# A third raw weight buffer, and g_final loaded into the output ring, in a one-layer hybrid encoder kernel

## The chip, the cores and the metric

The kernel runs on one core of one Trainium2 chip. A core has a matrix engine (TensorE, in the profile PE, with its weight loads as PEld), a vector engine (VectorE, DVE), a scalar engine (ScalarE, ACT), a general engine (GpSimd, POOL), and a queue engine (SyncE, SP) that in this kernel issues all transfers. Each engine carries out its own list of instructions in order and waits on semaphores for the others. The metric is the time of one execution on the device in microseconds, given as the median of several runs.

## What is computed

One inference step of a one-layer encoder over 2048 prompt tokens and 32 sample tokens that have 128 cached tokens before them. The model width is 1024, all numbers are fp32:

```python
a = rmsnorm(x, g_attn)
qa, ka, va, qb, kb, vb = split(a @ w_in)              # six parts of 512 columns
oa = softmax(q1 k1) v - lam * softmax(q2 k2) v        # group A: 4 heads, two maps, T5 bias, 64-chunk causal
ob = softmax(q k + clip bias) v                       # group B: 8 heads, own chunk and 8 chunks before
h = x + concat(rmsnorm(oa, subln_g) * c, rmsnorm(ob, out_norm_b)) @ w_out
h = h + square(relu(rmsnorm(h, g_mlp) @ w_up)) @ w_down          # 4096 wide
h = h + sigmoid(h @ w_ple_gate) * (p @ w_ple_proj)
y = rmsnorm(h, g_final)                               # outputs: y, and the new keys and values
```

The last line is the one that uses `g_final`: a vector of 1024 numbers, multiplied onto every token's row.

## The kernel before

**Tokens and precision.** The 2080 tokens are worked on in four blocks: 0, 1 and 2 of 512 tokens and 3 of 544 (its last 32 are the sample). To reach fp32 accuracy on TensorE, every operand is split into a high and a low part, and a product is three matmuls (`mm3`, L164 to L170): high weight by high activation (L168), high weight by low activation (L169), low weight by high activation (L170).

**Weights.** All weights are streamed in slices of 128 x 1024 numbers (512 KB, or 4 KB in each of the 128 partitions). `wunit` (L155) fetches one slice: a raw tile `wr` is loaded by SyncE, ScalarE copies it to the high part `wh` (L149), and GpSimd subtracts to get the low part `wl` (L153). There are 338 such slices in the run. The tiles come from rings: `wr` has two buffers, `wh` and `wl` three each. A raw buffer is free for the next load when both the copy and the subtraction of its slice are done; a `wh` or `wl` buffer is free when TensorE has finished the last matmul with it.

**Stages.** In order: normalisation and projection of blocks 0 and 1 (`prep`, `proj`, w_in); first half of attention A (`attn_a`, L516); projection and band attention (`attn_b`, L650) side by side; second half of attention A, into whose gaps the output projection (`outproj`, L818, w_out) and the MLP (`mlp`, L899 to L960, w_up and w_down) of blocks 0 and 1 are woven; then gate (`gate`, L966) and final norm (`final`, L1017) of block 1; output projection of blocks 2 and 3; gate and final norm of block 0; the MLP of blocks 2 and 3, which is nearly pure matrix work; and gate and final norm of blocks 2 and 3 at the end. In the profile, matmuls carry the names of their outputs: `qps` for w_in, `ops` for w_out, `ups` and `dps` for w_up and w_down, `gps` and `pps` for the gate, `s` for the scores of attention A (L545).

In attention A, keys (`ka`), queries (`q`) and values (`v`) are loaded from scratch memory in HBM for each head and group of queries. Its normed outputs `os` (L645) are stored back to HBM as `oT`.

**What sets the order.** All engines' instruction lists are written by a scheduler: the program is given to a tile framework (L1269) that places every instruction by priorities, buffers and a model of the times. A change of one buffer count can therefore move instructions on every engine. On the chip each list is then carried out in order, whatever the true times are. All transfers are issued by one line (`dma`, L139 to L144) on SyncE, so they stand in one queue: a transfer that has to wait for its buffer or its data holds back all transfers behind it.

**The final norm.** `final` is called four times, for the blocks 1, 0, 2 and 3 in this order. For each 128 tokens it transposes the block's hidden state on TensorE, copies it to a tile `yn` of 128 x 512 for each half of the columns (the last call uses the PSUM tile and an output tile `yo` for the second half), sums the squares into a throw-away tile `junk`, and multiplies by the row's scale and by `g_final` (L1054); then `yn` is stored. The tiles `yn`, `yo` and `junk` come from a ring of activation tiles with the tag "u": for block 1 the ring `uq` with 8 slots of 2 KB per partition, afterwards the ring `uh` with 16 slots. `g_final` lies in a tile `gf` of 128 x 1024 (4 KB per partition), the same row in each partition. `gfin` (L962) loads it, once into the pool `fk` before the second half's output projection (L1164), and once more into a new pool after block 1 is done (L1206).

Of the kernel before, what the change touches and what calls it, by code (L numbers as in the profile page):

```python
# [12 lines left out]
F32 = mybir.dt.float32  # L13
# [6 lines left out]
P = 128  # L20
D = 1024
# [12 lines left out]
BLK = 544  # L34
# [10 lines left out]
def toks(b):  # L45
    out = []
    for i in range(4):
        out.append((i * P, P))
    if b == 3:
        out.append((512, SS))  # L50
    return out
# [81 lines left out]
class Kern:  # L133
# [20 lines left out]

    def wunit(self, src, shape, hi_eng="act", lo_eng="pool"):  # L155
        nc = self.nc
        raw = self.wp.tile([P] + shape, F32, tag="wr", bufs=2, name="wr")
        self.dma(raw, src)
        hi = self.wp.tile([P] + shape, F32R, tag="wh", bufs=3, name="wh")
        lo = self.wp.tile([P] + shape, F32R, tag="wl", bufs=3, name="wl")  # L160
        self.split(hi, lo, raw, hi_eng, lo_eng)
        return hi, lo
# [796 lines left out]
            prev = us  # L959
        self.mlp_down(ch, nf, blocks, prev, st, wk, md)  # L960

    def gfin(self, pool):  # L962
        self.gf = pool.tile([P, D], F32, name="gf")
        self.dma(self.gf, self.a["g_final"].unsqueeze(0).broadcast_to([P, D]))

    def gate(self, b, h, up, act, md):  # L966
        nc, a = self.nc, self.a
        n, t0 = BN[b], 512 * b
# [48 lines left out]
    def final(self, b, h, up, fk, mm, md=None):  # L1017
        nc, a = self.nc, self.a
        t0 = 512 * b
        sts, yns = {}, {}  # L1020
        phased = md is not None

        def side(c0, tn, q):
            if phased:
                sts[c0] = st_all[:, c0 // P]
            elif q == 0:
                sts[c0] = fk.tile([P, 2], F32, tag="fst", bufs=6, name="fst")
            st = sts[c0]
            yp = (md if phased and q == 1 else mm).tile([P, 512], F32, tag="mm", name="yp")
            for k in range(4):  # L1030
                nc.tensor.transpose(yp[:tn, P * k : P * k + P], h[:, 4 * q + k, c0 : c0 + tn], self.ident)
            if phased and q == 1:
                yns[c0, q] = yp
            else:
                yns[c0, q] = up.tile([P, BLK], F32, tag="u", name="yn")[:, :512]
                nc.vector.tensor_copy(yns[c0, q][:tn], yp[:tn])
            junk = up.tile([P, BLK], F32, tag="u", name="junk")[:tn, :512]
            nc.scalar.activation(junk, yp[:tn], AF.Square, accum_out=st[:tn, q : q + 1])

        if phased:  # L1040
            st_all = fk.tile([P, 5, 2], F32, tag="fsa", name="fsa")
            nc.gpsimd.memset(st_all, 1.0)
            for c0, tn in toks(b):
                side(c0, tn, 0)
                yield
        def emit(c0, tn, r):
            tt = t0 + c0
            dst = a["y_prompt"][0, tt : tt + tn] if tt < SP else a["y_sample"][0, tt - SP : tt - SP + tn]
            for q in range(2):
                src = yn = yns[c0, q]  # L1050
                if phased and q == 1:
                    yn = up.tile([P, BLK], F32, tag="u", name="yo")[:, :512]
                g = self.gf[:tn, 512 * q : 512 * q + 512]
                nc.vector.scalar_tensor_tensor(yn[:tn], src[:tn], r, g, op0=ALU.mult, op1=ALU.mult)  # L1054
                self.dma(dst[:, 512 * q : 512 * q + 512], yn[:tn])

        if phased:
            for c0, tn in toks(b):
                side(c0, tn, 1)
            ss = fk.tile([P, 5], F32, tag="fss", name="fss")  # L1060
            nc.vector.tensor_tensor(ss, st_all[:, :, 0], st_all[:, :, 1], op=ALU.add)
            r = self.rsqrt(fk, ss, 5, 1.0 / D, EPS, nc.vector, "rfa")
            for i, (c0, tn) in enumerate(toks(b)):
                emit(c0, tn, r[:tn, i : i + 1])
            return
        for c0, tn in toks(b):
            side(c0, tn, 0)
            side(c0, tn, 1)
            st = sts[c0]
            nc.vector.tensor_tensor(st[:tn, 0:1], st[:tn, 0:1], st[:tn, 1:2], op=ALU.add)  # L1070
            emit(c0, tn, self.rsqrt(fk, st[:tn, 0:1], 1, 1.0 / D, EPS, nc.vector, "rf", tn, 5))
            yield

    def run(self):
        tc, nc, a = self.tc, self.nc, self.a
        with ExitStack() as top:

            def opened(stack, name, bufs, space=None, side="left"):
                kw = {} if space is None else {"space": space}
                return stack.enter_context(  # L1080
                    tc.tile_pool(name=name, bufs=bufs, side=side, reuse_waits="tile", **kw)
                )
# [31 lines left out]
            with ExitStack() as x:  # L1114
                pool = opened(x, "a0", 1, side="right")
# [42 lines left out]
            with ExitStack() as x:  # L1158
                pool = opened(x, "a1", 1, side="right")
# [1 line left out]
                    self.attn_a(js, pool, ps_s, ps_t, ps_o)  # L1161
            wk = opened(sq_, "wk", 1)
            fk = opened(sq_, "fk", 1)
            self.gfin(fk)  # L1164
            acc, cn, st = {}, {}, {}
            def norms(b, act, ps):
                self.colnorm(acc[b][0], b, 1.0 / D, wk, ps, "mm", self.rS)
# [10 lines left out]
            up = Sized(opened(top, "uh", 16, side="right"), BLK)  # L1178
# [24 lines left out]
            psx.close()  # L1203
            wk = opened(top, "wk4", 1)
            fk = opened(top, "fk4", 1)
            self.gfin(fk)  # L1206
            md = opened(top, "md", 8 - MM, PSUM, "right")
            act = Sized(opened(top, "acth", 4), BLK, True)
            hh = opened(top, "hh", 2, side="right")
# [1 line left out]
            g = self.outproj(3, wk, oa[3], md, acc[3])  # L1211
# [4 lines left out]
            g = self.gate(0, h, up, act, md)  # L1216
# [12 lines left out]
            g = self.gate(3, st[3][0], up, act, md)  # L1229
# [54 lines left out]
```

## Time and profile before

| | us |
|---|---|
| median of 3 runs | 3329.38 |
| lowest and highest run | 3328.49, 3332.86 |
| the profiled execution | 3334.02 |
| its span on the core | 3332.1 |

The mean granted clock of TensorE in the profiled execution was 0.969 of full speed. The profiled execution took 1.9 us beyond its span.

How the page is read: the busy table gives each engine's busy time, its share of the span and the number of its instructions. A group line names the source line, the engine, the operation and output<-input tiles, then the count, the busy total in us, the mean ns of one, and the idle time of the engine before these instructions with what ended most of it. A line of waits names who waited for whom, with the total in us, the number of times, and the longest. A line of the timeline begins with the start and the duration in us, and x2 means that two like instructions are merged into it; on SyncE a duration is that of issuing, together with waits between merged issues.

### The profile page before, as it was taken

The numbers are of one execution on the slowest core, as the hardware profiler recorded it, in microseconds if no ns is written. First come the engines' busy times: TensorE is split into PE (matmuls) and PEld (weight loads), VectorE is DVE, ScalarE is ACT, GpSimd is POOL, SyncE is SP. The second block draws the span as 40 slices with busy tenths as digits, with TensorE's granted clock in tenths as the row PEclk, the third lists the DMA queues.
The fourth block names the chain that finished last, engine by engine and source line by source line (L and its number), as shares of the span: only waits on it lengthen the run. The fifth ranks groups of instructions, "written<-read, shape, count | busy, mean of one in ns | idle before, by whom it ended". The sixth has DMA issues, their size and how long they took to land.

```text
span 3332.1 us, 50114 instructions
## 1 busy us (share of the span) xinstructions
PE 3111.6 (93%) x17881; PEld 2723.4 (82%) x17881; DVE 1674.4 (50%) x3952; ACT 1705.5 (51%) x3717; POOL 1467.9 (44%) x1083
## 2 busy tenths in 40 slices
PE   6988989999999999989899999988989999999998
PEld 6877778889877888778787878877779999999987
DVE  5117777454555544566656665746542322223235
ACT  4226666566665666666666665654443223222245
POOL 4335654432324433534544443555753333333365
PEclk9998899999999999999999999999999999999999
DMA  7488777786788554544644454346631111111133
GB/s 227 160 253 235 214 212 202 213 241 205 209 238 234 159 139 126 143 137 133 197 134 123 129 136 130 121 135 222 181 114 51 45 45 45 45 47 49 45 91 102
DMA packets 519074, 488.93 MB, mean 147 GB/s; under 512 B 37885, under 2 KB 414017, under 8 KB 518825
## 3 DMA queue, kind: packets, MB, share of 16 engines
q1 hardware_dynamic: 518824, 485.73, 50.2%
q8 instruction: 142, 2.33, 0.3%
q14 instruction: 108, 0.88, 0.1%
HBM read 379.06 MB, written 110.49 MB: 147 GB/s over the span
## 4 chain that ended last, share of the span: by engine, by line
PE 71%; DMA 12%; DVE 7%; ACT 3%; issue 3%; POOL 2%; SPq 2%; DVEq 0%; POOLq 0%; ACTq 0%
PE dps L168 6%; PE dps L169 6%; PE dps L170 6%; PE ups L168 6%; PE ups L169 6%; PE ups L170 6%; PE s L545 3%; DMA q<-qS 3%; PE qps L168 3%; PE qps L169 3%; PE qps L170 3%; PE ob L744 2%; PE sb L704 2%; SPq L144 2%; DMA ka<-kS 2%
## 5 line engine op out<-in xcount | busy, mean ns | idle before, releaser
L153 POOL TENSOR_TENSOR wl<-wr,wh 128x1024 fp32r<-128x1024 f32 x338 | 819.8, 2427 | 1027.5 <-ACT wh L149 985.3
L949 DVE TENSOR_TENSOR h<-h,dps 128x512 f32<-128x512 f32 (+1 forms) x640 | 373.1, 585 | 590.9 <-PE dps L170 578.4
L149 ACT ACTIVATE wh<-wr 128x1024 fp32r<-128x1024 f32 x338 | 357.4, 1058 | 539.9 <-PE dps L169 294.8
L168 PE MATMUL dps<-uh,wh 128*128 128x512 f32 (+1 forms) x1280 | 460.6, 360 | 14.8 <-DVE h L949 11.1
L168 PE MATMUL ups<-cH,wh 128*128 128x512 f32 (+1 forms) x1280 | 452.5, 354 | 9.3 <-ACT relu L914 7.7
L170 PE MATMUL dps<-uh,wl 128*128 128x512 f32 (+1 forms) x1280 | 453.0, 355 | 0.0
L169 PE MATMUL dps<-ul,wh 128*128 128x512 f32 (+1 forms) x1280 | 453.0, 354 | 0.0
L170 PE MATMUL ups<-cH,wl 128*128 128x512 f32 (+1 forms) x1280 | 451.9, 353 | 0.0
L169 PE MATMUL ups<-cL,wh 128*128 128x512 f32 (+1 forms) x1280 | 451.9, 353 | 0.0
L168 PEld LDWEIGHTS dps<-uh,wh 128*128 128x128 f32 x1280 | 243.8, 190 | 49.8 <-DVE h L949 16.9
L168 PEld LDWEIGHTS ups<-cH,wh 128*128 128x128 f32 x1280 | 242.2, 189 | 41.3 <-ACT relu L914 7.9
L170 PEld LDWEIGHTS dps<-uh,wl 128*128 128x128 f32 x1280 | 242.9, 190 | 33.4
L169 PEld LDWEIGHTS ups<-cL,wh 128*128 128x128 f32 x1280 | 242.7, 190 | 31.1
L153 POOL TENSOR_TENSOR ul<-relu,uh 128x272 fp32r<-128x272 f32 (+1 forms) x160 | 176.0, 1100 | 206.3 <-ACT uh L149 203.6
L170 PEld LDWEIGHTS ups<-cH,wl 128*128 128x128 f32 x1280 | 242.3, 189 | 30.1
L169 PEld LDWEIGHTS dps<-ul,wh 128*128 128x128 f32 x1280 | 243.2, 190 | 27.0
L545 PE MATMUL s<-ka,q 128*128 128x256 f32 (+4 forms) x784 | 197.2, 357 | 50.4 <-DMA q<-qS 29.1
L168 PE MATMUL qps<-aH,wh 128*128 128x512 f32 (+1 forms) x640 | 230.2, 360 | 6.6 <-ACT wh L149 2.2
L169 PE MATMUL qps<-aL,wh 128*128 128x512 f32 (+1 forms) x640 | 228.3, 357 | 0.0
L170 PE MATMUL qps<-aH,wl 128*128 128x512 f32 (+1 forms) x640 | 227.9, 356 | 0.0
L559 ACT ACTIVATE e<-s,nm 128x512 f32<-128x512 f32 (+3 forms) x256 | 155.2, 611 | 102.7 <-DVE nm L551 65.2
L545 PEld LDWEIGHTS s<-ka,q 128*128 128x128 f32 (+1 forms) x784 | 137.4, 200 | 78.5 <-issue 27.3
(217 smaller groups left out, 7076.9 us busy)
## 6 DMA issues: line engine op xcount, KB each, us to landing
wr<-w_up SPq DMA_DIRECT2D x96, 512.0 KB, 4.2
wr<-w_down SPq DMA_DIRECT2D x96, 512.0 KB, 3.7
wr<-w_in SPq DMA_DIRECT2D x74, 512.0 KB, 4.9
q<-qS SPq DMA_DIRECT2D x256, 128.0 KB, 4.7
v<-vSa SPq DMA_DIRECT2D x64, 512.0 KB, 3.8
ka<-kS SPq DMA_DIRECT2D x32, 512.0 KB, 7.2
wr<-w_out SPq DMA_DIRECT2D x32, 512.0 KB, 5.0
wr<-w_ple_gate SPq DMA_DIRECT2D x32, 512.0 KB, 4.4
```

The source lines that it names most:

```text
L144: self.nc.sync.dma_start(dst, src)
L149: nc.scalar.activation(hi, raw, AF.Copy)
L153: eng.tensor_tensor(lo, raw, hi.bitcast(F32), op=ALU.subtract)
L168: nc.tensor.matmul(ps, lh, rh, start=start and i == 0, stop=False)
L169: nc.tensor.matmul(ps, lh, rl, start=False, stop=False)
L170: nc.tensor.matmul(ps, ll, rh, start=False, stop=stop and i == n - 1)
L545: nc.tensor.matmul(s, q[:, m, hl, P * qi : P * qi + nr], kt[:, m, k0 : k0 + n], start=hl == 0, stop=hl == 1)
L559: nc.scalar.activation(dst, src, AF.Exp, bias=nmx, accum_out=z[:nr, m, bi : bi + 1])
L704: nc.tensor.matmul(s, q[:, 0, hl, P * qi : P * qi + nr], kt[:, c : c + w], start=hl == 0, stop=hl == 1)
L744: nc.tensor.matmul(o[:, qa:qb], vt, pt[:kn, i - kfirst, qa:qb], start=x == 0 and y == 0, stop=x == len(order) - 1 and y == 1,)
L949: nc.vector.tensor_tensor(hv, hv, ps, op=ALU.add)
```

## The change

The raw tile `wr` gets three buffers where it had two, which takes 4 KB more in each partition for the whole run. The tile `gf` of 4 KB and the method `gfin` with its two calls are gone. Instead `final` takes two tiles of 512 columns from the ring of its outputs at each of its four calls and loads one half of `g_final` into each. So `g_final` is loaded eight times in halves of 256 KB, where it was loaded twice in 512 KB.

```diff
@@ wunit
-        raw = self.wp.tile([P] + shape, F32, tag="wr", bufs=2, name="wr")
+        raw = self.wp.tile([P] + shape, F32, tag="wr", bufs=3, name="wr")
@@
-    def gfin(self, pool):
-        self.gf = pool.tile([P, D], F32, name="gf")
-        self.dma(self.gf, self.a["g_final"].unsqueeze(0).broadcast_to([P, D]))
@@ final
         phased = md is not None
+        gf = []
+        for q in range(2):
+            gf.append(up.tile([P, BLK], F32, tag="u", name="gf")[:, :512])
+            self.dma(gf[q], a["g_final"][512 * q : 512 * q + 512].unsqueeze(0).broadcast_to([P, 512]))
@@ emit, in final
-                g = self.gf[:tn, 512 * q : 512 * q + 512]
+                g = gf[q][:tn]
@@ run, before the woven output projection of blocks 0 and 1
-            self.gfin(fk)
@@ run, after the final norm of block 1
-            self.gfin(fk)
```

## The prediction

> **What bounds the kernel now.** I read the page's busy table first, then the stretches of the span, the groups of instructions, the waits, and the timeline of SyncE's queue.
>
> ```profile
> span 3332.1 us, 50114 instructions
> ...
> PE 3111.6 (93%) x17881; PEld 2723.4 (82%) x17881; DVE 1674.4 (50%) x3952; ACT 1705.5 (51%) x3717; POOL 1467.9 (44%) x1083
> ...
> PEclk9998899999999999999999999999999999999999
> ...
> L153 POOL TENSOR_TENSOR wl<-wr,wh 128x1024 fp32r<-128x1024 f32 x338 | 819.8, 2427 | 1027.5 <-ACT wh L149 985.3
> ...
> L149 ACT ACTIVATE wh<-wr 128x1024 fp32r<-128x1024 f32 x338 | 357.4, 1058 | 539.9 <-PE dps L169 294.8
> ```
> ```profile
> 1420.00:2210.00 790.00, 739.93 (x3714) 620.02 (x3713) 497.68 (x1047) 483.92 (x1115) 362.74 (x263) 0.97 0.48 134
> ...
> 2500.00:3300.00 800.00, 797.81 (x4932) 723.36 (x4931) 242.31 (x459) 256.85 (x458) 313.70 (x210) 1.00 0.18 56
> ```
>
> TensorE is busy for 3111.6 us of the 3332.1 us span; some 220 us are idle. A row of stretches gives length, busy time of PE, PEld, DVE, ACT and POOL (with counts), the granted clock, the DMA share and GB/s. The last 800 us of matrix work lose only 2.2 us (800.00 − 797.81) at clock 1.00: nothing is to be won there by a deeper weight buffer. So the change can act only before 2500 us.
>
> A weight slice goes through three steps: SyncE loads it (512 KB), ScalarE copies it to `wh` (1.06 us), GpSimd subtracts to `wl` (2.43 us). The raw buffer is the third of them to come free, after `wl`. What does ScalarE wait for before it writes `wh`?
>
> ```profile
> ACT wh L149 <- PE dps L169: 294.8, 39, 10.6
> ...
> ACT wh L149 <- PE ups L169: 61.3, 35, 4.4
> ...
> ACT wh L149 <- DMA wr<-w_in: 19.7, 12, 5.3
> ...
> ACT wh L149 <- DMA wr<-w_up: 17.8, 3, 7.9
> ...
> ACT wh L149 <- DMA wr<-w_out: 6.7, 3, 3.7
> ...
> ACT wh L149 <- DMA wr<-w_down: 4.4, 3, 2.4
> ```
>
> Columns: total us, times, longest. The first two, 356.1 us, are the healthy case: ScalarE is so far ahead that it waits for TensorE to free a `wh` slot. The last four, 48.6 us in 21 waits, are raw slices that came late. Only these can a third raw buffer shorten. How much of the 48.6 us reaches TensorE is read from the stretches in which they lie:
>
> ```profile
> 222.00:242.00 20.00, 18.61 (x77) 14.74 (x78) 4.40 (x9) 7.71 (x13) 11.54 (x7) 0.92 0.98 305
> 252.00:264.00 12.00, 10.26 (x50) 7.90 (x49) 3.64 (x13) 5.57 (x15) 3.86 (x3) 1.00 0.96 282
> ...
> 601.00:611.00 10.00, 9.77 (x78) 9.55 (x78) 3.50 (x4) 4.03 (x8) 8.35 (x7) 1.00 0.48 144
> 646.00:656.00 10.00, 7.41 (x46) 6.74 (x46) 4.71 (x14) 6.28 (x15) 3.94 (x2) 0.80 0.99 256
> 1364.00:1378.00 14.00, 11.21 (x44) 8.17 (x43) 5.14 (x11) 7.16 (x16) 5.71 (x4) 0.92 1.02 267
> 1625.00:1651.00 26.00, 25.05 (x134) 21.16 (x133) 7.32 (x18) 13.42 (x27) 10.87 (x7) 1.00 1.04 319
> ```
>
> TensorE's idle time (length less PE busy) is 1.39, 1.74, 0.23, 2.59, 2.79 and 0.95 us: 9.69 us in all. In five of the six the DMA share is 0.96 to 1.04: the slices are late because every DMA engine is full, not because they were asked for late.
>
> **The change, part by part.**
>
> *Third raw buffer.* It adds no instruction. Load n+1 now stands in SyncE's queue where load n stood, and waits for the same event, the `wl` of unit n−2. So what is blocked behind it is what was blocked before, and only the content is one unit ahead: on entering a full stretch, one more slice of 512 KB has landed. It is worth what those bytes take at that stretch's rate, and no more than the idle time: 512 KB (524,288 bytes) at 305, 282, 256, 267 and 319 GB/s is 1.72, 1.86, 2.05, 1.96 and 1.64 us. The smaller of the two in each: 1.39 + 1.74 + 0.23 + 2.05 + 1.96 + 0.95 = **8.3 us**. With the idle time the clock should recover. Its loss is 0.08 × 20 + 0.20 × 10 + 0.08 × 14 = 4.7 us; I take half, 2.4 us, because attention's own gaps lie in the same stretches. Bounds for this part: 0 if the order shifts put something else there; 9.7 + 4.7 = 14.4 us if all goes.
>
> [...]
>
> *The orders that the planner moves.* All engines' orders are planned, so a buffer moves more than itself. In the two instruction lists side by side, TensorE's 17,876 matmuls and loads are the same in number; the order is identical up to index 1198 and, but for tiny swaps, after about 2245 us. Between 1000 and 2212 us the weight work (outproj, MLP up and down) runs 10 to 70 matmuls ahead of the attention pieces. SyncE's list differs where second-half attention A changes to new keys:
>
> ```profile
> 1436.42 0.58 SPq L144 DMA_DIRECT2D ka<-kS  x1
> 1439.41 0.35 SPq L144 DMA_DIRECT2D oT<-os  x1
> 1439.80 2.33 SPq L144 DMA_DIRECT2D ka<-kS  x2
> ...
> 1517.25 1.24 SPq L144 DMA_DIRECT2D ka<-kS  x2
> ...
> 1521.88 1.08 SPq L144 DMA_DIRECT2D oT<-os  x1
> ...
> 1702.91 1.23 SPq L144 DMA_DIRECT2D ka<-kS  x2
> ...
> 1707.53 0.59 SPq L144 DMA_DIRECT2D oT<-os  x1
> ```
> ```profile
> 1436.81 2.57 DVE L645 SCALAR_TENSOR_TENSOR os<-os,g_sub_s,rsy 128x256 f32<-128x256 f32 x1 [1.03 <-POOL rsy L182]
> ...
> 1521.04 0.81 DVE L645 SCALAR_TENSOR_TENSOR os<-os,g_sub_s,rsy 128x256 f32<-128x256 f32 x1
> ...
> 1706.23 0.48 DVE L645 SCALAR_TENSOR_TENSOR os<-os,g_sub_s,rsy 128x256 f32<-128x256 f32 x1
> ```
> ```profile
> 1519.00:1535.00 16.00, 12.10 (x48) 9.39 (x47) 10.80 (x21) 4.83 (x11) 5.26 (x5) 0.82 0.89 211
> ...
> 1702.00:1728.00 26.00, 21.93 (x106) 18.22 (x105) 11.85 (x26) 13.73 (x29) 12.76 (x11) 0.93 0.80 179
> ```
>
> At the first boundary the store of `os` now stands behind the key and query loads; before, it held two key loads until DVE's `os` was done (1439.38), while the load ahead of it went at 1436.42 and took 0.58: 2.4 us won, at most. At the second and fourth the store is moved ahead of the key loads (at the third a store of `h` is). If it waits for the same `os` end, the keys leave at 1521.85 instead of 1517.25 and at 1706.71 instead of 1702.91: 4.6 and 3.8 us later, with the query loads, the next raw slices and TensorE's in-order score matmuls behind them. Net 4.6 + 3.8 − 2.4 = 6.0 us. Its cover is the weight work that now stands ahead: 10 to 70 matmuls at 0.162 us (797.81 / 4932) is 1.6 to 11.3 us. That can hide none or all; I take half, **3.0 us lost**, ends 0 and 6.0, and more with the clock, which the two rows show at 0.82 and 0.93 when TensorE waits there. Three of four groups whose query loads were split around such a store are whole now; I give that no price, its lower bound is the group wait in the rivals.
>
> *g_final in the output ring.* Removed: two loads of 512 KB. Added: eight of 256 KB, two in each of the four calls.
>
> ```profile
> L144 SPq DMA_DIRECT2D gf<-g_final x2: 333/421/509, 909.2 to 2249.0; - x2
> ...
> DMA to landing us min/median/max: 4.1/4.3/4.5
> ```
> ```profile
> 2268.38 1.02 SPq L144 DMA_DIRECT2D y_prompt<-yn  x2
> ...
> 2276.28 3.15 SPq L144 DMA_DIRECT2D y_prompt<-yn  x2
> ...
> 3290.09 33.92 SPq L144 DMA_DIRECT2D y_prompt<-yn  x3
> ```
> ```profile
> 3322.89 0.75 DVE L1054 SCALAR_TENSOR_TENSOR yn<-yn,rsy,gf 128x512 f32<-128x512 f32 x1
> ```
>
> For the last call the loads stand ahead of its first output store, so they are out by about 3290, land some 4.3 us later, and are first needed at 3322.89: covered by 28 us. The loads of calls 0 and 2 lie in matrix work at DMA share 0.18. In call 1 the same 512 KB is moved, and two of eight ring slots are taken; its blocks of tokens come 7.9 us apart (2276.28 less 2268.38), and each takes four slots, so with six left one is needed again one and a half blocks later. I take 0; the ends are 0 and 3 us, the latter if each of the three other calls delays a raw load behind it by two issues of up to 0.509 us. What becomes late if this cover goes is the gate of that block, through the raw loads queued behind.
>
> *Start.* The third slice is asked for in the first microseconds, when SyncE waits for an activation buffer anyway, and its `wl` moves into a gap of GpSimd. I take 0, with ± 2 us (one `wl`, 2.43 us, beside or ahead of the norms).
>
> **Sum.** −8.3 − 2.4 + 3.0 + 0 + 0 = −7.7 us. The profiled execution took 3334.0 us (span 3332.1 and 1.9 around it), so it would take 3326.3. It lies 4.6 us over the median of the runs, 3329.4; against that: **3321.7, said as 3322 us.**
>
> **Rivals.**
> - *Slower: the store blocks the keys.* The two delays reach TensorE whole (8.4 us), the clock dips in those rows grow by as much again as they are now (0.18 × 16 + 0.07 × 26 = 4.7 us), and what was to be won is paid back by full DMA engines, because the slice that comes early takes the bandwidth of the same keys and queries. 3329.4 + 8.4 + 4.7 = 3342.5. It decides when less than 1.6 us of weight work stands behind the last score of a group. For it: TensorE already idles 3.9 of 16 us and 4.1 of 26 us there. Against it: the 10 to 70 matmuls. [...]
>
> ```profile
> SPq L144 <- POOL wl L153: 1214.8, 221, 16.3
> ...
> SPq L144 <- DVE os L645: 79.7, 20, 9.2
> ```
>
> - *More is won.* The whole 14.4 us and, where query groups are no longer split, most of the row below, which ends a chain through the same queue: 3329.4 − 14.4 − 10 = about 3305, where the 10 is a third of that row. The order that the planner gives speaks for it; that the row was not caused by raw slices speaks against it.
>
> ```profile
> PE s L545 <- DMA q<-qS: 29.1, 12, 4.1
> ```
>
> - *It does not do what it says.* With `wh` limited to three slots, 356.1 us of waits say that TensorE sets the pace of weights, and 1214.8 us say that raw loads stand waiting for `wl`; the late slices are late from bandwidth, and an earlier request changes nothing: 3329 us, within 6.7.
>
> **How the numbers follow.** No change is told from one below about 0.2% (6.7 us). Forecast case 0.44, its own range 3314 to 3328, of which 0.32 lies beyond 0.2% and 0.12 within; more is won 0.14; nothing 0.08; slower 0.34. So faster 0.32 + 0.14 = 0.46, same 0.12 + 0.08 = 0.20, slower 0.34. The range takes in the larger gain down to 3304 (leaving 0.06 below) and the slower rival with 3 us for the ring up to 3346 (leaving 0.14 above).
>
> **What would show it.** Right: the waits of ScalarE on raw slices fall from 48.6 us to under 25; the six stretches' counterparts lose most of 9.7 us of idle time; TensorE's idle time falls from 220 to about 212 us, all of it before 2500 us; the `gf` group shows eight loads landed long before their use. Wrong: the wait of score matmuls on queries or keys grows beyond 29.1 us, or SyncE's on `os` beyond 79.7; idle time appears between 1500 and 2212 us or in the stage of 2210 to 2500 us, whose last call's stores free the memory that the next stage's tiles take.

## The result, and the profile after

The changed kernel takes 3315.76 us (median of 5 runs, 3314.81 to 3318.08) against 3329.38 us: a ratio of 0.9957, 95% interval 0.9944 to 0.9971, or 14 us less (10 to 19). On a second chip the same pair gave 0.9957 again (0.9942 to 0.9973). The forecast was 3322 us, faster by 7.7.

The page and the waits of the changed kernel, from an execution of 3318.08 us:

```profile
span 3316.2 us, 50119 instructions
...
PE 3103.1 (94%) x17881; PEld 2715.9 (82%) x17881; DVE 1681.4 (51%) x3952; ACT 1698.8 (51%) x3717; POOL 1468.2 (44%) x1083
```
```profile
ACT wh L149 <- PE dps L169: 288.0, 39, 10.6
...
ACT wh L149 <- PE ups L169: 69.5, 42, 2.9
...
PE s L545 <- DMA q<-qS: 33.7, 14, 6.1
...
PE gps L168 <- ACT wh L149: 10.1, 2, 9.6
...
ACT wh L149 <- DMA wr<-w_in: 4.0, 2, 3.2
```

The last line is all that is left of ScalarE's waits on raw slices: 4.0 us where there were 48.6. The waits on TensorE (357.5 us in the first two lines, 356.1 before) are as they were. TensorE's idle time, span less busy time, is 213.1 us, from 220.5. So the buffer did what it says. But where TensorE gained is another question, and the stretches (length, busy time of five engines, clock, DMA share, GB/s) answer it. They are the counterparts of those at 222, 252, 646, 1364 and 1625 us before, with partly other matmuls in them:

```profile
216.00:236.00 20.00, 18.40 (x76) 14.48 (x77) 5.00 (x10) 7.38 (x13) 9.69 (x8) 0.90 1.03 322
247.00:259.00 12.00, 11.79 (x56) 9.55 (x55) 4.11 (x16) 5.71 (x17) 3.69 (x2) 1.00 1.06 301
...
639.00:649.00 10.00, 8.54 (x69) 8.10 (x67) 4.07 (x16) 6.03 (x13) 3.69 (x3) 1.00 1.04 294
1351.00:1365.00 14.00, 11.38 (x46) 8.58 (x45) 4.56 (x7) 5.12 (x9) 7.43 (x6) 0.94 1.03 235
1606.00:1632.00 26.00, 23.73 (x114) 20.11 (x113) 10.62 (x23) 15.38 (x31) 11.67 (x8) 0.93 1.06 286
```

Two stretches are better: that at 640 us, with 69 matmuls in ten microseconds at clock 1.00, where there were 46 at 0.80, and that at 247 us, which is idle for 0.21 us instead of 1.74. That at 216 us idles 1.60 us against 1.39, that at 1351 us is as idle as before (2.62 us against 2.79), and that at 1606 us is worse (2.27 us against 0.95). The DMA engines are as full as they were: a share of 1.03 to 1.06 in these five, 0.96 to 1.04 in the five before.

Two executions of one program can differ by several microseconds in one stage, so I took a trace of the kernel before (run b0_before) and one of the changed kernel (a0_changed) on one chip, another than that of the page above. The end of the n-th matmul (counted from 0) in both traces gives a table of stages:

| matmuls (us, kernel before) | before | changed | difference |
|---|---|---|---|
| to 500 (start, to 98 us) | 98.5 | 98.7 | +0.2 |
| 500 to 8000 (to 1468) | 1369.4 | 1365.2 | −4.2 |
| 8000 to 11,000 (second half of attention A, to 2109) | 641.2 | 624.9 | −16.3 |
| 11,000 to 13,000 (gate, norm, output projection, to 2524) | 414.4 | 415.4 | +1.0 |
| 13,000 to the last (to 3312) | 788.1 | 788.5 | +0.4 |

On the first chip the same rows are −5.5, −7.9, −5.1, +1.3 and +0.7. There the kernel before spent 102.1 us on the start, and 98.5 on the other chip; the changed kernel spent 96.6 and 98.7. So most of that −5.5 is a difference of two executions.

Both pairs agree that the stages from 500 to 11,000 gain, and that the stage behind them loses a little. How the gain divides is less certain, because the planner puts somewhat different work under the numbers 8000 and 11,000. The numbers 7849 and 11,464 have the same matmuls, by output and shape, ahead of them in both kernels. From 500 to 7849 the difference is −9.9 us on the first chip and −4.8 on the other; from 7849 to 11,464, nearly all of the second half of attention A, it is −2.5 and −14.6. So the large gain of the second half stands in one pair of traces. Its row in both traces of the one chip, kernel before first, and then its waits of the scores on queries:

```profile
1468.00:2109.00 641.00, 600.97 (x3001) 502.55 (x3000) 405.34 (x845) 389.14 (x901) 291.94 (x215) 0.97 0.49 138
```
```profile
1464.00:2089.00 625.00, 592.44 (x3002) 495.54 (x3001) 410.00 (x845) 385.31 (x894) 289.16 (x213) 0.99 0.50 141
```
```profile
PE s L545 <- DMA q<-qS: 22.7, 9, 4.3
```
```profile
PE s L545 <- DMA q<-qS: 11.5, 7, 3.1
```

Nearly the same 3000 matmuls need 8.5 us less busy time (the clock is 0.99, from 0.97) and 7.5 us less idle time, and the waits on queries are halved. ScalarE waits 7.6 us on raw slices there before, and 1.6 us after. On the first chip the waits on queries are halved as well (23.8 to 12.5 us), but the busy time is no less (597.2 and 598.1 us, both at clock 0.98).

Over the whole run the waits on queries did not fall. They are 29.1 us before and 33.7 after on the first chip, and 27.6 in both kernels on the other: what the second half saves comes back in the stages ahead of it, with waits of 6.1 us at 362 us and 3.2 at 298 in the changed kernel.

One place in the second half where such a wait fell is a change of query groups under the same keys; the kernel before first (the score matmul's row, then the stretch around it), then the changed kernel:

```profile
1754.75 0.70 PE L545 MATMUL s<-ka,q 128*128 128x512 f32 x2 [3.25 <-DMA q<-qS]
```
```profile
1752.00:1760.00 8.00, 5.25 (x17) 4.38 (x18) 6.44 (x9) 3.50 (x6) 2.97 (x2) 0.79 0.45 111
```
```profile
1745.96 0.70 PE L545 MATMUL s<-ka,q 128*128 128x512 f32 x2 [0.31 <-DMA q<-qS]
```
```profile
1743.00:1751.00 8.00, 7.69 (x39) 6.18 (x38) 7.27 (x13) 4.61 (x11) 3.69 (x2) 1.00 0.45 140
```

In brackets stands the idle time before the matmul and what ended it: 3.25 us became 0.31. Both kernels load the four queries here in one piece, so it is not the splitting of query groups that went. In the changed kernel TensorE has weight work to do while the queries travel: 39 matmuls in 8 us, against 17. The queries also come sooner there. In the kernel before, the load of a weight slice goes out just ahead of theirs (at 1748.00 us), in the changed kernel just behind (1744.17), and the score matmul starts 3.7 and 1.9 us after the last query load is out.

### The profile page after: what moved, and what is told of

Same layout as the page of the kernel before. It is cut to its first block, busy times and chain, and to the rows that moved or that the text cites. A ratio compares the mean times of both kernels' runs of the same rounds, so it can differ in the third digit from the quotient of the medians.

```text
span 3316.2 us, 50119 instructions
## 1 busy us (share of the span) xinstructions
PE 3103.1 (94%) x17881; PEld 2715.9 (82%) x17881; DVE 1681.4 (51%) x3952; ACT 1698.8 (51%) x3717; POOL 1468.2 (44%) x1083
## 4 chain that ended last, share of the span: by engine, by line
PE 51%; DMA 6%; DVE 5%; ACT 2%; issue 1%; POOL 1%; SPq 1%; DVEq 0%; POOLq 0%; ACTq 0%
PE dps L168 6%; PE ups L168 6%; PE ups L169 6%; PE ups L170 6%; PE dps L169 6%; PE dps L170 6%; DMA q<-qS 3%; PE s L545 3%; PE gps L168 1%; PE gps L169 1%; PE gps L170 1%; PE tpp L617 1%; PE ob L744 1%; DVE e L582 1%; PE o L632 1%
## 5 line engine op out<-in xcount | busy, mean ns | idle before, releaser
L168 PEld LDWEIGHTS ups<-cH,wh 128*128 128x128 f32 x1280 | 241.5, 189 | 45.8 <-ACT relu L914 10.2
L545 PE MATMUL s<-ka,q 128*128 128x256 f32 (+4 forms) x784 | 195.7, 352 | 47.6 <-DMA q<-qS 33.7
L559 ACT ACTIVATE e<-s,nm 128x384 f32<-128x384 f32 (+3 forms) x256 | 154.9, 610 | 85.7 <-DVE nm L551 67.8
```

The costliest lines, as they stand in the source:

```text
L168: nc.tensor.matmul(ps, lh, rh, start=start and i == 0, stop=False)
L545: nc.tensor.matmul(s, q[:, m, hl, P * qi : P * qi + nr], kt[:, m, k0 : k0 + n], start=hl == 0, stop=hl == 1)
L559: nc.scalar.activation(dst, src, AF.Exp, bias=nmx, accum_out=z[:nr, m, bi : bi + 1])
```

## The experiments

Ratios are to the kernel before on the same chip, with 95% intervals. Every kernel is planned anew, so each differs from the others in its order too.

**The ring alone.** Two raw buffers, `g_final` in the output ring:

```diff
-        raw = self.wp.tile([P] + shape, F32, tag="wr", bufs=3, name="wr")
+        raw = self.wp.tile([P] + shape, F32, tag="wr", bufs=2, name="wr")
```

> g_final in the output ring, but two raw buffers as before. Theory (the third raw buffer carries the gain: late raw slices go): within 4 us of the kernel before, 3326 to 3333 us, and the waits of ScalarE on raw slices stay near 48 us. Rival (the gain is that of the ring and of the other memory and order that go with it): 3314 to 3321 us.

Measured: 1.0012 (1.0003 to 1.0022), 4 us slower, with 41.8 us of waits on raw slices (21.7 on w_up, 10.0 on w_out, 7.7 on w_in, 2.4 on w_down). The ring by itself brings no gain; with the order that goes with it, this kernel is a little slower.

**Which slices need it.** Here the raw tile rotates over single buffers, with a depth by the number of the slice; a rotation over three, or over two, gives the order of the ring of three, or of two.

```diff
-        nc = self.nc
-        raw = self.wp.tile([P] + shape, F32, tag="wr", bufs=3, name="wr")
+        u = self.units = getattr(self, "units", -1) + 1
+        self.slot = (getattr(self, "slot", -1) + 1) % (2 if u < 8 else 3)
+        raw = self.wp.tile([P] + shape, F32, tag=f"wr{self.slot}", bufs=1, name="wr")
```

That is the run e2_start_two. The others have `3 if u < 8 else 2` (e3_start_only), `3 if u >= 128 else 2` (e4_late_only), `3 if 8 <= u < 128 else 2` (e5_mid_only) and `2 if 8 <= u < 128 else 3` (e10_not_mid).

> The changed kernel, but the first 8 slices (the first projection) rotate over two raw buffers; all later ones over three. Theory: the start loses the 5.5 us by which the changed kernel's 500th matmul ended earlier (96.6 against 102.1 us), so 3320 to 3323 us, with the 500th matmul at about 102 us. Rival (the start's gain is swallowed by a later wait): 3314 to 3318 us.

> Three raw buffers for the first 8 slices only, two for all later ones, g_final in the ring. Theory: the start's 5.5 us alone, 3322 to 3326 us, and the 500th matmul at about 96.6 us. Rival (the start's gain is swallowed later): 3327 to 3332 us.

> Two raw buffers up to slice 127, three from slice 128 on (the second half of attention A and all after it), g_final in the ring. Theory: no gain before about 1340 us and 4 to 7 us after, 3322 to 3326 us. Rival (the gain of that half was a luckier order of the planner's, not the buffer): anything from 3315 to 3340 us, without relation to the waits on raw slices after 1340 us, which are gone here as in the changed kernel.

The next two are the trace pair of the section above. e5_mid_only ran on their chip, e10_not_mid on another:

> The kernel before, for a trace from the chip on which the three kernels beside it run. Every theory expects the time of the runs of the kernel before on this chip.

> The changed kernel once more, on another chip. Theory and rivals alike: a ratio of 0.994 to 0.997; against the trace of the kernel before from the same chip, the start gains 5 to 6 us by the 500th matmul if the third buffer does it, and 2 us if that gap was a difference of two executions.

> Three raw buffers for slices 8 to 127 alone (projections, first half of attention A, band attention, output projection and the first MLP chunks), two before and after, g_final in the ring. If the parts add up (ring +4, start -7, late -6, each from its own run against the ring alone), the rest of the change's -14 us is this part: some 5 us less than the ring alone, a ratio of about 0.9995. If the middle carries most of it (the kernel without the third buffer at the start lost nothing), 11 us less than the ring alone: 0.997 to 0.9985.

> Three raw buffers for slices 0 to 7 and from 128 on, two for slices 8 to 127, g_final in the ring. If the middle slices carry the gain: 0.998 to 1.001 of the kernel before. If any third buffer that changes the order can bring it: 0.994 to 0.997. The loss of the slices around 646 us is back in either case: about 10 us for these 46 matmuls, where three buffers take 5.5.

Measured; the second column gives the raw buffers for slices 0 to 7, 8 to 127 and from 128 on, the last two are stages of the table above, in us. Each stage is from one trace, and those of e1 to e4 and of e10 come from two other chips; the two traces of the changed kernel alone give 624.9 and 632.3 us in the last column, those of the kernel before 641.2 and 637.4.

| run | buffers | ratio (interval) | matmuls 500 to 8000 | 8000 to 11,000 |
|---|---|---|---|---|
| b0_before (`gf` in its tile) | 2 2 2 | 1 | 1369.4 | 641.2 |
| e1_ring_only | 2 2 2 | 1.0012 (1.0003 to 1.0022) | 1363.7 | 643.3 |
| e3_start_only | 3 2 2 | 0.9990 (0.9979 to 1.0000) | 1382.4 | 627.3 |
| e4_late_only | 2 2 3 | 0.9995 (0.9981 to 1.0009) | 1357.9 | 638.3 |
| e10_not_mid | 3 2 3 | 1.0001 (0.9991 to 1.0012) | 1382.7 | 627.7 |
| e2_start_two | 2 3 3 | 0.9961 (0.9945 to 0.9977) | 1359.2 | 631.5 |
| e5_mid_only | 2 3 2 | 0.9953 (0.9936 to 0.9969) | 1357.9 | 627.2 |
| a0_changed | 3 3 3 | 0.9957 (0.9942 to 0.9973) | 1365.2 | 624.9 |

The ratios fall into two groups. Whoever has three buffers for slices 8 to 127 (projections, band attention, output projection, first MLP chunks: 70 to 1340 us) gains 0.4 to 0.5%; whoever has not is within 0.12% of the kernel before, even with three everywhere else. The start is not needed: e2_start_two is as fast without it, and its 500th matmul, expected at 102 us, ended at 99.4. Still, over all traces of this document the 500th matmul ends at 98.5 to 102.3 us in the eight traces with two buffers there (mean 100.2) and at 96.6 to 99.3 in the six with three (mean 98.0), so some 2 us may be won at the start and lost again later. The parts do not add up either. My first expectation of e5_mid_only, 0.9995, is false, and the second, 0.997 to 0.9985, was too cautious. And against the ring alone on the same chip, e3_start_only and e4_late_only are 7 and 5 us faster, so a third buffer outside the middle is not without effect.

The last column is the more telling one. It should be short where the *late* slices have three buffers. It is not: e4_late_only has them and is long; e3_start_only and e5_mid_only have two there and are short, by 11 us, which is more than the 7 us between two executions. Three buffers at that place are neither needed for the gain nor, by this one trace, enough for it. What these kernels also differ in is the order of the planner, which a buffer given long before changes.

Kernels with the short second half but two buffers in the middle (e3_start_only, e10_not_mid) lose as much before: 1382 us, against 1358 to 1368 with three. Not every order with two is so slow (1357.9 in e4_late_only), so the buffer does not set that stage by itself.

The numbers 500, 3140, 11,564 and 13,000 have the same matmuls ahead of them in every kernel of this document, and say more exactly where the kernels part (us, one trace each, with both traces of the kernel before and the changed one):

| run | buffers | 500 to 3140 | 3140 to 11,564 | 11,564 to 13,000 |
|---|---|---|---|---|
| kernel before | 2 2 2 | 507.7, 502.3 | 1627.6, 1629.7 | 294.7, 293.0 |
| e1_ring_only | 2 2 2 | 502.8 | 1625.8 | 298.5 |
| e3_start_only | 3 2 2 | 512.8 | 1618.0 | 291.4 |
| e4_late_only | 2 2 3 | 499.9 | 1617.9 | 306.0 |
| e10_not_mid | 3 2 3 | 513.1 | 1615.8 | 297.0 |
| e2_start_two | 2 3 3 | 492.6 | 1617.2 | 298.9 |
| e5_mid_only | 2 3 2 | 490.8 | 1613.7 | 294.8 |
| changed kernel | 3 3 3 | 507.9, 502.4 | 1611.6, 1606.1 | 298.7, 297.1 |

From 3140 to 11,564 every kernel with a third buffer anywhere is faster than those without, by 8 us or more, where two executions of one kernel differ by 2 to 6. e3_start_only and e10_not_mid have lost as much by 3140 as they win then; e2_start_two and e5_mid_only have won as much again, at a place where the changed kernel wins nothing; and e4_late_only loses its share at the end. That the middle slices carry the gain is thus true of the end times, but not shown as a cause.

At one place the slices themselves are seen to act. The 45 matmuls 3405 to 3449, which end at 656 us in the kernel before, take 10.2 and 10.5 us in its two traces, and 9.6 to 9.7 us in e1_ring_only and e3_start_only; with three buffers for the middle they take 5.5 to 5.6 us in every kernel. Expected of e10_not_mid were about 10 us; it took 7.4, and e4_late_only, with two, 5.6. So this stall too can be avoided by order. These numbers hold partly other matmuls with three buffers: over 3398 to 3476, which have the same ones, the changed kernel gains 1.9 us on the first chip and 4.6 on the other. The stretch in e3_start_only, and in a0_changed:

```profile
645.00:655.00 10.00, 7.70 (x50) 7.03 (x48) 5.01 (x14) 6.81 (x16) 4.28 (x3) 0.83 0.97 264
```
```profile
637.00:643.00 6.00, 6.00 (x51) 6.00 (x51) 2.94 (x11) 3.92 (x9) 1.47 (x1) 1.00 1.05 303
```

**The queries early.** The second half of attention A waits on queries, which stand behind up to six loads of keys (at 1817.76 us in the kernel before, six that take 4.58 us to issue, and the queries at 1822.38). Its loads in another order:

```diff
-            for hl in range(2):
-                src = self.kS[g, hl].rearrange("(m r) c -> r m c", m=2)
-                for c0 in range(0, nk, 1024):
-                    c1 = min(c0 + 1024, nk)
+            q = None
+            for c0 in range(0, nk, 1024):
+                c1 = min(c0 + 1024, nk)
+                for hl in range(2):
+                    src = self.kS[g, hl].rearrange("(m r) c -> r m c", m=2)
                     self.dma(kt[64 * hl : 64 * hl + 64, :, c0:c1], src[:, :, c0:c1])
+                if q is None:
+                    q = self.load_q(pool, g, 256 * js[0], 256, (0, 1))
```

The pair function takes this `q` for the first group of queries and loads the others itself. The edit changes two things, the order of the keys and the place of the queries, and no run parts them. Three kernels with it: on top of the changed one (e7_q_early, and again as e11_q_early_again on another chip), on the kernel before (e8_before_q_early), and on the ring with two raw buffers (e9_ring_q_early).

> The changed kernel with the loads of attention A in another order: both head halves of the first 1024 keys, then the first queries, then the rest of the keys (before: all keys of one half, all of the other, then the queries). Theory (the scores' 33.7 us of waits on queries are the time of the keys ahead of them in the queue): 10 to 20 us faster than the changed kernel, 0.990 to 0.993 of the kernel before. Rival (the DMA engines are full there, and the same bytes come later elsewhere): 0.994 to 0.997, as the changed kernel.

> The kernel before (two raw buffers, g_final in its tile) with only the order of the loads of attention A changed: first 1024 keys of both halves, then the first queries, then the other keys. Theory (what the second half of attention A gained in the changed kernel was time of waits on queries, by the order of SyncE's queue, and not raw slices): waits of scores on queries fall from 27.6 us to under 8, and the time to 0.990 to 0.996 of the kernel before with no third buffer. Rival (raw slices): the waits move to the raw slices, 0.997 to 1.001.

> The same load order with g_final in the ring and two raw buffers: against the kernel of the next but one run it differs in the third buffer alone. If the third buffer's own worth is what the stretches with late slices lost (4 to 10 us), it is 4 to 10 us slower than that one. If it acted through the planner's order alone, within 3 us of it.

> The changed kernel with the queries early once more, on the chip of the three runs beside it: 0.990 to 0.993 of the kernel before by its first run; every theory expects that.

Measured: 0.9915 (0.9897 to 0.9933) and, repeated, 0.9918 (0.9899 to 0.9937), or 28 us less than the kernel before: it beats both kernels. On the kernel before alone 0.9959 (0.9945 to 0.9974); with the ring and two buffers 0.9986 (0.9970 to 1.0002). The second half's row of e11_q_early_again and its waits on queries, then those of e9_ring_q_early:

```profile
1465.00:2080.00 615.00, 588.04 (x3003) 491.57 (x3002) 411.68 (x840) 387.19 (x892) 291.35 (x213) 1.00 0.51 143
```
```profile
PE s L548 <- DMA q<-qS: 3.5, 3, 1.5
```
```profile
1468.00:2097.00 629.00, 595.27 (x3006) 497.78 (x3004) 404.59 (x843) 387.49 (x895) 293.89 (x216) 0.98 0.50 140
```
```profile
PE s L548 <- DMA q<-qS: 16.9, 8, 5.3
```

The waits on queries go with the length of this stage: as they go from 22.7 over 16.9 and 11.5 to 3.5 us, the 3000 matmuls go from 641 over 629 and 625 to 615 us. They do not set it alone: with waits of 16 to 17 us it takes 627 us in e5_mid_only and 638 in e4_late_only. In e8_before_q_early they fell over the whole run only to 18.3 us, not under 8 as expected, yet its time came out as the theory had it. e9_ring_q_early differs from it by the ring alone and is 7 us slower, so the ring, with its order, costs something here too. Between e9_ring_q_early and e11_q_early_again lies the third buffer alone, and it is worth 0.7% there, more than the 4 to 10 us that I expected; 13 us of it (628.1 against 614.9) fall in this stage, where a short wait on a slice is hardly the reason, since e5_mid_only has such waits there (16.2 us on w_up) and is fast.

Whether the third buffer helps by its slices or only by letting the planner put weight work where queries travel stays open: no run had the changed kernel's order with two buffers, since the planner makes an order for each.

## Why the prediction was right, point by point

- **Third raw buffer, −8.3 us and −2.4 us of clock.** Late slices went as told (48.6 to 4.0 us), but TensorE kept most of the idle time in those stretches. Over the shortest ranges of numbers around the first five that hold the same matmuls in both kernels, the stretches at 222, 252, 601, 646 and 1364 us changed by −0.7, −0.8, −0.5, −1.9 and −0.4 us, −4.3 in all, on the first chip, and by +0.2, −0.9, −0.1, −4.6 and +1.6, −3.8 in all, on the second, where these five should have given 7.4 us and the clock. (Around 1625 us no short range of this kind exists.) The failed step is the bound "no more than the idle time": I took the idle time of a stretch for the late slice's. The timeline before says what ended it. Of the 9.7 us, 2.18 are a wait on the slice's copy (at 651 us), and 1.39 and 2.56 more waits on ScalarE, which did its work behind a late copy. The other 3.6 us are waits on VectorE (2.0 us) and on queries (1.5 us), which a raw buffer does not end by itself. First two lines of this, from the kernel before, then what stands in the counterparts at 1351 and 1606 us, where TensorE now waits on queries instead:

```profile
1374.36 1.17 PE L545 MATMUL s<-ka,q 128*128 128x384 f32 x4 [2.56 <-ACT e L559]
1630.93 1.50 PE L545 MATMUL s<-ka,q 128*128 128x512 f32 x6 [0.90 <-DMA q<-qS]
```
```profile
1362.25 1.98 PE L545 MATMUL s<-ka,q 128*128 128x512 f32 x6 [2.54 <-DMA q<-qS]
1625.01 0.70 PE L545 MATMUL s<-ka,q 128*128 128x512 f32 x2 [2.27 <-DMA q<-qS]
```

- **Order, +3.0 us.** TensorE's idle time within 15 us before and after the first score matmul on new keys, summed over the eight changes of keys, is 27.2 us before and 25.9 after on one chip (28.7 and 25.5 on the other). At the four changes that the step looked at it is 15.1 and 16.0 (16.8 and 16.0): won at the first, as told, lost at the fourth, and about nothing in sum. So the 3 us were not lost. The step counted the stores and keys alone. The "10 to 70 matmuls" of weight work, which I used only as a cover for that loss, can also cover the queries of the groups between, as at 1746 us above; the stage as a whole gained 3 to 15 us over the same matmuls. Both halves of my sum were off, in opposite directions.
- **g_final in the ring, 0 (0 to 3 us).** The eight loads land 3.5 to 6.7 us after their issue. But the kernel with the ring alone is 4 us slower, just over the bound, and 7 us with the queries early. In e1_ring_only 4.8 us against b0_before lie from the 11,500th to the 12,000th matmul (120.5 against 115.7), and in the output projection TensorE waits 7.6 us for VectorE's `hd` (L838) over the run, against 2.7. Yet e3_start_only, with the same ring, takes 111.3 us there. So the ring does not cost this by itself, and the order remains as a cause that was not tried.
- **Start, 0 ± 2.** Within its bounds on one chip (0.2 us later), outside on the other (5.5 us earlier); the mean over all traces, some 2 us earlier, lies at the bound, and a kernel without it ends no later.
- **Slower, by stores ahead of keys.** The stalls at the changes of keys did not grow, where 8.4 us were told, so the rival fell.
- **More is won, 3305 us.** Fell: 10 to 19 us were won, not 24. The waits on queries, of which it took a third, did not fall over the whole run. With the queries loaded early 28 us are won, more than it told, by another change.
- **It does not do what it says.** Fell: the intervals exclude no change.
- **What would show it.** Idle time was told as 212 us and was 213. "All of it before 2500 us" held: the matmuls from 13,000 on take 0.4 to 0.7 us more. The six stretches did not lose most of their idle time. And two of the signs of being wrong came: the waits of scores on queries grew from 29.1 to 33.7 us, SyncE's on `os` from 79.7 to 82.5, and yet the kernel is faster. Not told was a wait that grew, the gate's first matmul on `wh`, from 7.4 to 9.6 us: in ScalarE's list that copy, which starts at 2379.88 us, stands behind copies that wait 3.16, 1.04 and 1.04 us for VectorE's `tmp` (L859).

So the sign and the size were right within a factor of two, and the reason only in part. That the sum came out near is partly luck: 10.7 us were promised where some 4 were won, and 3 us of loss where there was a gain.

## What to carry to other kernels

Where a planner writes the order, a buffer can be worth what the new order is worth: compare where the work moved, not only the waits that the buffer ends, and test it by giving the buffer to one stage at a time. A wait that ends on a transfer is first a question of what stands ahead of it in the queue: moving the queries ahead of half of the keys, and with them the order of the keys, gave as much here as the whole change (0.9959 and 0.9957), and took no memory. Before idle time is priced, look up what ends it, matmul by matmul. And before a stage's difference is believed, take two traces of the same program: the start took 102.1 and 98.5 us in two executions of the kernel before.

## What the runs showed of the hardware

The granted clock was lower after some stalls of 2 to 4 us. Run b0_before, stretches around one stall at 520 us and one at 1994 us; the idle time, length less the first busy time, is 1.72 and 3.30 us. The third row has as much idle time as the first, 1.84 us, and no loss of clock:

```profile
518.00:524.00 6.00, 4.28 (x14) 3.41 (x15) 5.68 (x24) 3.30 (x10) 2.14 (x3) 0.72 1.03 264
```
```profile
1990.00:1999.00 9.00, 5.70 (x19) 4.48 (x18) 7.74 (x11) 4.19 (x8) 3.61 (x2) 0.81 0.52 133
```
```profile
1470.00:1476.00 6.00, 4.16 (x19) 3.09 (x18) 3.57 (x6) 3.74 (x8) 5.67 (x5) 1.00 0.52 141
```

The clock's loss is 0.28 × 6 = 1.7 us in the first row and 0.19 × 9 = 1.7 us in the second. In the second it shows in the matmuls: those with 512 columns start 0.23 us apart from 1994.15 to 1994.61 us, and 0.43 us apart from 1994.98 to 1996.26. The trace of the kernel before from the first chip shows how long it lasts: the granted clock is 0.50 from 529.16 to 532.57 us, after a stall of 2.00 us that ended at 528.47 (with others of 0.57 us before it and 0.20 behind), and 0.50 from 2000.30 to 2003.71 us, after a stall of 3.62 us that ended at 1999.80. So in the stretch around 520 us TensorE loses as much by the clock, 1.7 us, as by standing idle, 1.72.

Not every such stall was followed by a loss: the third row, with one of 1.77 us, has clock 1.00, and so has the first chip's trace from 1472 to 1492 us, around a stall of 2.16 us at 1481. Why they differ is not shown. That half of the clock's loss in the stretches with late slices would go was my estimate. Their five counterparts in the changed kernel lose 0.10 × 20 + 0.06 × 14 + 0.07 × 26 = 4.7 us, as the stretches before did, with partly other matmuls in them. In the traces of the second chip the second half of attention A gained as much in busy time (8.5 us, at a clock of 0.99 where it was 0.97) as in idle time (7.5 us).
